# Two-layer decoder trunk: the norm's matrix of 1/1024 moved 64 bytes along its tile, and three 16-column products put ahead of query projections

## The chip, the cores and the metric

One core of a Trainium2 chip runs the whole program. The time is the device time of one execution in microseconds; for the kernel before, three executions gave 1483.13, 1483.56 and 1486.03 us, and the median is 1483.56 us. One more execution was profiled. In what follows PE is the matrix engine, DVE, ACT and POOL are the vector, scalar and GpSimd engines, and SP is the engine that issues most transfers.

## What is computed

A trunk of two layers over 512 tokens of width 1024, batch 1, all in float32. Each layer is a token mixer and a gated feed-forward network with a causal convolution; each of the two is led by an RMS norm that is shifted and scaled by a conditioning vector, and its output is gated and added to the residual stream. The first mixer is retention with four heads, the second an mLSTM with four heads; both have query and key width 256 and value width 512 per head.

```python
for i in range(DEPTH):
    h = rmsnorm(x, norm_tok_g[i]) * (1.0 + sc_t) + sh_t
    y = retention_mixer(h, ...) if i % 2 == 0 else mlstm_mixer(h, ...)
    x = x + gt_t * y
    h = rmsnorm(x, norm_ffn_g[i]) * (1.0 + sc_f) + sh_f
    x = x + gt_f * conv_ffn(h, ...)
return rmsnorm(x, final_g)
```

## The kernel before

**Products.** The residual stream lies in SBUF as eight tiles of 128 channels by 512 tokens. Every float32 operand of a large product is split into a rounded high part and a low part (names that end in h and l, or `whi` and `wlo`), and a product is three matmuls: high by high, high by low, low by high. Most large projections use a seven-product (Strassen-like) scheme: a matrix pair is cut in quarters and seven products of 128x256 columns in four steps take the place of eight (`ORDER`, `seven`, `fold_pairs`, `fold_values`). So the bulk of PE's work is matmuls of 256 moving columns; other stages (output projections, the first head's projections) use 512 columns, and the scores and their application mix 512, 384 and 256.

**Names on PE.** `p` is a folded projection, weights `whi` or `wlo` stationary and token tiles (`hh`, `hl`, `t24h`, `t3h`, ...) moving; `pv` is a folded value projection, token tiles stationary and weights moving; `po` is an output or down projection; `pf` are the first four products behind a norm; `psc` and `pav` are scores and their application; `pmu` and `pvar` are the two products of a head's group norm, with the matrix `ones_v`; `pms` are the two products of an RMS norm (or of its half), with the matrix `ones_d`, all entries 1/1024, stationary and the split sum of squares `ssh`, `ssl` moving.

**Where operands begin.** A token tile ("slot") is 512 words, 2048 bytes per partition, and is used from its first byte, or from its middle. A weight tile is 1024 + 64 words, 4352 bytes, and the folded weights, and those of the boundary at a norm, are used from word `OFF` = 16, 64 bytes in. `ones_d`, `ones_v` and `ones_1` are 128 words each and are used from their first byte; in the built program `ones_d` begins at byte 4352 of each partition, a multiple of 128.

**Boundaries.** At the end of a mixer or of a feed-forward network (`boundary`), the last output products run in two halves of 256 tokens, so that the first half's norm can start while the second half is multiplied. `Norm.root` issues the two `pms` products of a half. In three of the four boundaries the second half's `po` products are followed by `pf` (192 matmuls in four parts), and then by products of 512 columns; the fourth ends the program.

**A product nobody reads.** `short_product` multiplies the first weights of what follows with 16 columns into a place of PSUM that is written over later. It stands already ahead of the two mixers' last boundary (`contract_tiles` with `lead`) and ahead of the first folded unit of each feed-forward network (`folded`).

**Order.** The program is recorded as calls, and a planner (`Plan`) lists them engine by engine: PE's calls by their place in the code, the others by due times that it works out from PE's, with an estimate `occ` for each call. PE's order may still interleave the end of one seven-product group with the start of the next, where operands are late by the plan.

The lines that matter: `ones` at 431 to 436, `short_product` at 659, `seven` at 821, `fold_pairs` at 850, `ret_q` at 1714 and `ml_q` at 1856. All engine instructions are issued at line 383.

Of the kernel before, what the change touches and what calls it, by code (L numbers as in the profile page):

```python
# [11 lines left out]
F32R = mybir.dt.float32r  # L12
# [4 lines left out]
P = 128  # L17
# [18 lines left out]
WPAD = 64  # L36
OFF = 16
# [349 lines left out]
def trunk(ctx: ExitStack, tc: tile.TileContext, xT, cb, pos, vec, ident, decay, zmask, ada, w_s0, w_in0, w_v0,  # L387
          w_o0, w_in1, w_v1, w_f1, w_o1, w_up, w_dn, out):
    nc = tc.nc
    const = ctx.enter_context(tc.tile_pool(name="const", bufs=1))  # L390
# [10 lines left out]
    def uid(s):  # L401
        count[0] += 1
        return f"{s}_{count[0]}"

    def tile_of(pool, shape, dt, tag, name):
        return Buf(pool, shape, dt, tag, name, KINDS.get(tag, 0), tag == "ps")

    def slot(s, dt=F32, w=T):
        return tile_of(slots, [P, w], dt, "s", uid(s))
# [10 lines left out]
    def fixed(pool, shape, dt, name):  # L420
        b = tile_of(pool, shape, dt, name, name)
        b.get()
        return b

    plan = Plan()
    V, A, G, PE, S = (plan.engine(*p) for p in (("DVE", nc.vector), ("ACT", nc.scalar), ("POOL", nc.gpsimd),
                                                ("PE", nc.tensor), ("SP", nc.sync)))
# [3 lines left out]
    V.memset(fixed(const, [P, 32], F32, "pad")[:], 0.0)  # L431
    ones = {}
    for name, v in (("d", 1.0 / D), ("v", 1.0 / DV), ("1", 1.0)):
        o = fixed(const, [P, P], F32R, f"ones_{name}")
        V.memset(o[:].bitcast(F32), v)
        ones[name] = o

# [221 lines left out]
    def short_product(o, w, b):  # L659


        PE.matmul(o, w, b, start=True, stop=True, skip_group_check=True)

    def mm2(o, w, b, r=slice(None), start=True, stop=True):
        PE.matmul(o, w, b.hi[:, r], start=start, stop=False)
# [89 lines left out]
    def item(uses, fn, free=True):  # L755
        for u in uses:
            if u.first is None:
                u.first = len(items)
            u.last = len(items)
        items.append((uses, fn, free))  # L760
        steps_at.append(now[0])
# [3 lines left out]
    def proj_item(src, h, then, added=False):  # L765
        def fn(w):
            ps = bank("pp")
            for k in range(KT):
                cs = slice(k * P, k * P + P)
                mm3(ps[:], w[0].hi[:, cs], w[0].lo[:, cs], h[k].hi[:], h[k].lo[:], k == 0, k == KT - 1)  # L770
            then(ps)
        item([Use(src, KT * P, added=added)], fn)
# [45 lines left out]
                PE.matmul(o, b[0][:, ts], lo[:, cs], start=False, stop=False, skip_group_check=True)  # L818
                PE.matmul(o, b[1][:, ts], hi[:, cs], start=False, stop=sp, skip_group_check=True)

    def seven(use, streams, done, between=lambda j: None):


        fs = []

        def mk(n):
            def fn(w):
                if n == ORDER[0]:
                    for s in streams:
                        s.open(w[0])  # L830
                        fs.append(slot("fs"))
                for s, f in zip(streams, fs):
                    o = {1: s.c21, 2: s.c11, 5: s.c12, 3: s.c12}.get(n, s.c21)
                    s.product(n, o, n in s.starts)
                    if n in (1, 6, 7):
                        A.copy(f[:, HB if n == 6 else HA], s.c21)
                    if n == 7:
                        V.tensor_tensor(s.c22, s.c12, f[:, HA], op=ALU.add)
                    elif n == 2:
                        V.tensor_tensor(s.c11, s.c11, f[:, HA], op=ALU.add)  # L840
                    elif n == 3:
                        V.tensor_tensor(s.c12, s.c12, f[:, HB], op=ALU.add)
                if n == 3:
                    done(*[s.banks for s in streams])
            return fn
        for j, n in enumerate(ORDER):
            item([use], mk(n), j in FREE_STEPS)
            between(j)

    def fold_pairs(srcs, terms, thens, between=lambda j: None):  # L850

        def each(then):
            def done(bs):
                for b in bs:
                    then(b)
            return done
        for n, (src, then) in enumerate(zip(srcs, thens)):
            seven(FoldUse(src, n), [PairStream(terms, then)], each(then), lambda j: between(7 * n + j))

    def fold_values(src, terms, v, split, between=lambda j: None):  # L860

        def done(a, b):
            for ps in (a[0], b[0], a[1], b[1]):
                split(v, ps)
        seven(ValueFoldUse(src, 0), [ValueStream(terms, t) for t in range(2)], done, between)

    def folded(folds, h, terms, pairs, downs, quota):
# [30 lines left out]
        def unit(i):  # L898
# [10 lines left out]
            if i == 0:  # L909
                short_product(c2[:, HB][:, :16], folds[0].p[1][0][:, :P], terms(1, 0)[0][:, :16])  # L910
# [124 lines left out]
    def contract_tiles(w, n, gate, ys, i, t0, t1, after=lambda m: None, js=None, lead=False):  # L1035

        r = slice(t0, t1)
        per = WCOLS // (n * P)
        for j in js or range(per):
            m = i * per + j  # L1040
            ps = bank("po")
            if lead:
                short_product(ps[:, T - 16 :], w.hi[:, :P], ys(0).hi[:, :16])
                lead = False
            for k in range(n):
                cs = slice((j * n + k) * P, (j * n + k) * P + P)
                la = w.lo_at(j * n + k, k)
                mm3(ps[:, r], w.hi[:, cs], w.lo[:, la : la + P], ys(k).hi[:, r], ys(k).lo[:, r], k == 0, k == n - 1)
            add_residual(ps, m, gate(m), t0, t1)
            after(m)  # L1050
# [464 lines left out]
    def half_pair(st, name, finish):  # L1515

        got = []

        def then(ps):
            got.append(ps)  # L1520
            if len(got) == 2:
                st[name] = finish(*got)
        return then
# [181 lines left out]
    sums0 = Sums(h0, {}, 0, 0)  # L1705

    def sums_early():
        sums0.make()
        sums0.turn()

    def pair_srcs(w, at):
        return [(w[at], w[at + 1]), (w[at + 2], w[at + 3])]

    def ret_q(i, between=nothing):
        thens = [half_pair(R[i], name, rope) for name in ("q", "k")]
        if i:
            fold_pairs(pair_srcs(w_in0, i * 8), sums0.terms, thens, between)
            return
        for n, then in enumerate(thens):
            for j in range(2):  # L1720
                proj_item(w_in0[i * 8 + 2 * n + j], h0, then, 2 * n + j in QLOW)
        item([], lambda w: sums_early())

    def ret_g(i):
        fold_pairs(pair_srcs(w_in0, i * 8 + 4), sums0.terms, [ret_gate(i)] * 2)
# [9 lines left out]
    def ret_o(i):  # L1735
        if not i:
            item([], lambda w: load_x())
        return pieces(lambda j: w_o0[i, j], 4, gate_col(0, 0), lambda k: R[i]["y"][k], i in O_ADDED)

    ffn0 = Ffn(0)  # L1740
    heads(R, ret_q, ret_v, ret_scores, ret_g, ret_attend, lambda i: None, ret_end, ret_o,
          ffn0.start, RET_LAST, "ret")

# [41 lines left out]
    def conv_then(i, name, kt):  # L1785
        ch = (0 if name == "q" else 8) + i * 2 + kt

        def then(ps):
            acc = slot("mc")[:]
            c = lambda j: col("mcw", j * 16 + ch)  # L1790
            A.activation(acc, ps[:], AF.Identity, bias=col("mcb", ch), scale=c(3))
            for j, s in ((2, 1), (1, 2), (0, 3)):
                V.scalar_tensor_tensor(acc[:, s:], ps[:, : T - s], c(j), acc[:, s:], op0=ALU.mult, op1=ALU.add)
            A.activation(acc, acc, AF.Silu)
            M[i][name].append(pair_of("mqk", acc))
        return then
# [22 lines left out]
    def ml_gate(i):  # L1819
        def then(ps):  # L1820
            o = slot("o")
            A.activation(o[:], ps[:], AF.Sigmoid)
            M[i]["o"].append(o)
        return then
# [30 lines left out]

    def ml_q(i, between=nothing):
        thens = [lambda ps, name=name, n=iter((0, 1)): conv_then(i, name, next(n))(ps) for name in ("q", "k")]
        fold_pairs(pair_srcs(w_in1, 1 + i * 8), start1.sums.terms, thens, between)

    def ml_g(i):  # L1860
        fold_pairs(pair_srcs(w_in1, 5 + i * 8), start1.sums.terms, [ml_gate(i)] * 2)
# [4 lines left out]
    def ml_v(i, between=nothing):  # L1866
        fold_values(w_f1[i - 1], start1.sums.terms, M[i]["v"], plain_split, between)

    start1 = Start([w_in1[j] for j in (0, 5, 6, 7)], h1, 1, 0, [gates, ml_gate(0), ml_gate(0), ml_gate(0)], True)
# [3 lines left out]
    item([], lambda w: start1.sums.turn())  # L1873
    ffn1 = Ffn(1)
    heads(M, ml_q, ml_v, ml_scores, ml_g, ml_attend, lambda i: gn_center(M[i]), ml_end, ml_o,
          ffn1.start, ML_LAST, "ml")
    ffn1.items(End())
# [145 lines left out]
```

## Time and profile before

| what | value |
|---|---|
| median of three executions | 1483.56 us |
| profiled execution, its own time | 1483.41 us |
| its span, first to last instruction | 1481.6 us |
| granted PE clock, mean | 0.997 |
| busy: PE, DVE, ACT, POOL | 99%, 86%, 73%, 19% of the span |
| chain that ended last: PE, DMA, DVE | 86%, 7%, 3% |

The span is 1.8 us shorter than the execution's own time. Matmuls overlap in the profile: a matmul of 256 columns is shown as some 280 ns long, but the next one starts 113 to 118 ns after it. So in the timeline the difference between two start times, divided by the number of matmuls from the one to the other, tells what a matmul costs; the busy time does not. In the timeline a row is: start, length, engine, line, operation, output and inputs, stationary size, moving size and type, how many, and in brackets how long the engine was idle before it and who ended that.

### The profile page before, as it was taken

The numbers are of one execution on the slowest core, as the hardware profiler recorded it, in microseconds if no ns is written. First come the engines' busy times: TensorE is split into PE (matmuls) and PEld (weight loads), VectorE is DVE, ScalarE is ACT, GpSimd is POOL, SyncE is SP. The second block draws the span as 40 slices with busy tenths as digits, with TensorE's granted clock in tenths as the row PEclk, the third lists the DMA queues.
The fourth block names the chain that finished last, engine by engine and source line by source line (L and its number), as shares of the span: only waits on it lengthen the run. The fifth ranks groups of instructions, "written<-read, shape, count | busy, mean of one in ns | idle before, by whom it ended". The sixth has DMA issues, their size and how long they took to land.

```text
span 1481.6 us, 27248 instructions
## 1 busy us (share of the span) xinstructions
PE 1461.3 (99%) x10468; PEld 1368.8 (92%) x10468; DVE 1268.1 (86%) x2136; ACT 1075.9 (73%) x1606; POOL 279.0 (19%) x313
## 2 busy tenths in 40 slices
PE   9999999999999999999999999999999999999997
PEld 6799999998999999999999998999889899999997
DVE  7999979777989889898897999999889887777786
ACT  5678768777577676676668986989856876767662
POOL 0334132322111111111001222132211111111100
PEclk9999999999999999999999999999999999999998
DMA  9868989888798899999457895888687887888751
GB/s 363 252 175 207 282 209 230 224 250 212 206 215 215 241 261 258 265 261 266 118 180 171 207 246 144 208 221 199 205 239 201 213 219 194 194 208 191 190 125 58
DMA packets 93268, 315.65 MB, mean 213 GB/s; under 512 B 12225, under 2 KB 14657, under 8 KB 93138
## 3 DMA queue, kind: packets, MB, share of 16 engines
q0 software_dynamic: 32112, 116.54, 42.2%
q1 hardware_dynamic: 60738, 197.11, 38.3%
q8 instruction: 82, 1.34, 0.4%
q10 hardware_dynamic: 288, 0.27, 0.1%
q14 instruction: 48, 0.39, 0.1%
HBM read 195.23 MB, written 2.12 MB: 133 GB/s over the span
## 4 chain that ended last, share of the span: by engine, by line
PE 86%; DMA 7%; DVE 3%; ACT 2%; issue 2%; POOL 0%; DVEq 0%; ACTq 0%; SPq 0%; POOLq 0%
PE p L383 36%; PE po L383 27%; PE pv L383 9%; PE pav L383 4%; PE pp L383 3%; PE pf L383 3%; DMA wlo<-raw 2%; PE psc L383 2%; DMA raw<-w_in 1%; DMA wb<-w_up 1%; DMA raw<-w_dn 1%; PE pst L383 1%; DMA wlo<-wa 1%; DMA raw<-w_up 1%; PE pms L383 1%
## 5 line engine op out<-in xcount | busy, mean ns | idle before, releaser
L383 PE MATMUL p<-hh,whi 128*128 128x256 f32 (+1 forms) x994 | 275.6, 278 | 1.9 <-DVE p L383 1.9
L383 PE MATMUL p<-hl,whi 128*128 128x256 f32 x992 | 275.1, 277 | 0.0
L383 PE MATMUL p<-hh,wlo 128*128 128x256 f32 x992 | 273.4, 277 | 0.0
L383 ACT ACTIVATE wlo<-whi 128x1024 fp32r<-128x1024 f32 x223 | 235.0, 1057 | 39.8 <-PE po L383 15.1
L383 PEld LDWEIGHTS p<-hh,whi 128*128 128x128 f32 x994 | 187.1, 188 | 2.8 <-DVE p L383 2.3
L383 PEld LDWEIGHTS p<-hl,whi 128*128 128x128 f32 x992 | 186.7, 188 | 0.4
L383 PEld LDWEIGHTS p<-hh,wlo 128*128 128x128 f32 x992 | 185.6, 188 | 0.0
L383 PE MATMUL p<-t24h,whi 128*128 128x256 f32 x744 | 165.0, 279 | 4.1 <-ACT fs L383 3.1
L383 PE MATMUL po<-ggl,whi 128*128 128x512 f32 (+1 forms) x448 | 153.3, 343 | 0.0
L383 PE MATMUL po<-ggh,wlo 128*128 128x512 f32 (+1 forms) x448 | 153.1, 343 | 0.0
L383 PE MATMUL po<-ggh,whi 128*128 128x512 f32 (+1 forms) x448 | 152.4, 343 | 0.0
L383 ACT CAST whi<-raw 128x1024 fp32r<-128x1024 f32 (+1 forms) x117 | 118.0, 1019 | 44.8 <-DMA raw<-w_s 10.5
L383 PE MATMUL p<-t24l,whi 128*128 128x256 f32 x496 | 137.5, 277 | 0.0
L383 DVE SCALAR_TENSOR_TENSOR x<-po,mod,x 128x512 f32<-128x512 f32 (+1 forms) x184 | 113.0, 628 | 23.2 <-PE po L383 22.7
L383 PEld LDWEIGHTS p<-t24h,whi 128*128 128x128 f32 x744 | 126.3, 188 | 6.9 <-ACT fs L383 3.9
L383 DVE SCALAR_TENSOR_TENSOR ada<-ada,c_ext 128x1025 f32<-128x1025 f32 x96 | 119.5, 1246 | 6.5 <-DMA ada<-ada 6.4
L383 POOL DMA_DIRECT2D wlo<-wa x62 | 53.8, 867 | 355.4 <-ACT wlo L383 223.4
L383 PE MATMUL po<-yh,whi 128*128 128x256 f32 (+1 forms) x354 | 116.0, 329 | 0.3 <-ACT o L383 0.3
L383 PE MATMUL po<-yl,whi 128*128 128x256 f32 (+1 forms) x352 | 115.7, 329 | 0.0
L383 PE MATMUL po<-yh,wlo 128*128 128x256 f32 (+1 forms) x352 | 115.6, 329 | 0.0
L383 DVE SCALAR_TENSOR_TENSOR cv<-p,vecs,cv 128x511 f32<-128x511 f32 (+1 forms) x144 | 106.4, 744 | 9.9 <-ACT cv L383 9.2
L383 ACT CAST whi<-ws 128x1024 fp32r<-128x1024 f32 x86 | 90.0, 1050 | 28.5 <-DVE ws L383 23.5
(287 smaller groups left out, 4422.0 us busy)
## 6 DMA issues: line engine op xcount, KB each, us to landing
ada<-ada SPq DMA_DIRECT2D x96, 512.5 KB, 7.4
wlo<-ws POOLq DMA_DIRECT2D x68, 512.0 KB, 6.9
wlo<-wa POOLq DMA_DIRECT2D x62, 512.0 KB, 6.3
wlo<-wt POOLq DMA_DIRECT2D x44, 512.0 KB, 6.9
wlo<-raw POOLq DMA_DIRECT2D x41, 512.0 KB, 8.4
wa<-w_up SPq DMA_DIRECT2D x36, 512.0 KB, 6.9
wb<-w_up SPq DMA_DIRECT2D x36, 512.0 KB, 6.2
raw<-w_o SPq DMA_DIRECT2D x32, 512.0 KB, 6.6
```

The source lines that it names most:

```text
L383: getattr(c.obj, c.name)(*[real(v) for v in c.a], **{key: real(v) for key, v in c.k.items()})
```

## The change

`ones_d` becomes a tile of 128 + 64 words, of which words 16 to 143 are used: the matrix begins 64 bytes later. Every SBUF tile that is allocated behind it moves up by 256 bytes. `seven` takes a flag `lead`; where it is set, the first of the seven products is preceded by one 16-column product with its first high weights and its first moving tile, into the second bank's other half (`c22`), which is written by a vector instruction later on. The planner counts it with `occ = 0`. The flag is set for the first of the two groups in `ret_q(2)`, `ml_q(0)` and `ml_q(2)`: the third retention head's queries, and the first and third mLSTM heads' queries.

```diff
     for name, v in (("d", 1.0 / D), ("v", 1.0 / DV), ("1", 1.0)):
-        o = fixed(const, [P, P], F32R, f"ones_{name}")
+        off = OFF if name == "d" else 0
+        o = fixed(const, [P, P + WPAD * (off > 0)], F32R, f"ones_{name}")[:, off : off + P]
         V.memset(o[:].bitcast(F32), v)
...
-        PE.matmul(o, w, b, start=True, stop=True, skip_group_check=True)
+        return PE.matmul(o, w, b, start=True, stop=True, skip_group_check=True)
...
-    def seven(use, streams, done, between=lambda j: None):
+    def seven(use, streams, done, between=lambda j: None, lead=False):
...
                         s.open(w[0])
                         fs.append(slot("fs"))
+                    if lead:
+                        hi, hc, _, _ = w[0].p[n]
+                        short_product(streams[0].c22[:, :16], hi[:, hc : hc + P],
+                                      streams[0].terms(n, 0)[0][:, :16]).occ = 0.0
...
-            fold_pairs(pair_srcs(w_in0, i * 8), sums0.terms, thens, between)
+            fold_pairs(pair_srcs(w_in0, i * 8), sums0.terms, thens, between, i == 2)
...
-        fold_pairs(pair_srcs(w_in1, 1 + i * 8), start1.sums.terms, thens, between)
+        fold_pairs(pair_srcs(w_in1, 1 + i * 8), start1.sums.terms, thens, between, i in (0, 2))
```

On PE, at the start of `ret_q(2)`: the last two rows of the first head's output projection (`po`, 512 columns), and then the query products. This is a piece of the difference, with + for the row that is new.

```order
 L383 MATMUL po_2142<-yl_1916,whi_1880 128x512
 L383 MATMUL po_2142<-yh_1903,wlo_2021 128x512
+L383 MATMUL p_415_2161<-hh_239,whi_1842 128x16
 L383 MATMUL p_415_2161<-hh_239,whi_1842 128x256
 L383 MATMUL p_415_2161<-hl_267,whi_1842 128x256
```

One row is added, with the operands of the row behind it; nothing else moves there. On PE, at the start of `ml_q(2)`, behind the group norm's two products for the second mLSTM head (`pmu`), the kernel before has

```order
L383 MATMUL po_10997<-yh_10835,wlo_10896 128x512
L383 MATMUL pmu_11020<-zsh_10942,ones_v 128x512
L383 MATMUL pmu_11020<-zsl_10951,ones_v 128x512
L383 MATMUL p_1846_11028<-hh_8793,whi_10763 128x256
L383 MATMUL p_1846_11028<-hl_8805,whi_10763 128x256
```

and the changed kernel has (buffer numbers are higher by one for each product added ahead)

```order
L383 MATMUL po_10999<-yh_10837,wlo_10898 128x512
L383 MATMUL pmu_11022<-zsh_10944,ones_v 128x512
L383 MATMUL pmu_11022<-zsl_10953,ones_v 128x512
L383 MATMUL p_1846_11030<-hh_8794,whi_10765 128x16
L383 MATMUL p_1846_11030<-hh_8794,whi_10765 128x256
L383 MATMUL p_1846_11030<-hl_8806,whi_10765 128x256
```

Again one row is added. The third such row stands at the start of `ml_q(0)`, behind the first head's value products (`pv`, 512 columns). Apart from these three rows every engine has the same instructions in the same order as before, transfers included.

More of the change, by code (lines that the diff above doesn't have):

```diff
@@ L848, in seven, with fold_pairs @@
             between(j)
-    def fold_pairs(srcs, terms, thens, between=lambda j: None):
+    def fold_pairs(srcs, terms, thens, between=lambda j: None, lead=False):
         def each(then):
@@ L857, in fold_pairs @@
         for n, (src, then) in enumerate(zip(srcs, thens)):
-            seven(FoldUse(src, n), [PairStream(terms, then)], each(then), lambda j: between(7 * n + j))
+            seven(FoldUse(src, n), [PairStream(terms, then)], each(then), lambda j: between(7 * n + j),
+                  lead and not n)
     def fold_values(src, terms, v, split, between=lambda j: None):
```

## The prediction

> **What bounds the kernel now.** I read the page first: the span, and how much of it PE is busy.
>
> ```profile
> span 1481.6 us, 27248 instructions
> PE 1461.3 (99%) x10468; PEld 1368.8 (92%) x10468; DVE 1268.1 (86%) x2136; ACT 1075.9 (73%) x1606; POOL 279.0 (19%) x313
> L383 PE MATMUL p<-hh,whi 128*128 128x256 f32 (+1 forms) x994 | 275.6, 278 | 1.9 <-DVE p L383 1.9
> ```
>
> PE is the bound nearly everywhere, so what a matmul costs in time from start to start decides. That is read from PE's timeline, by the first and the last row of a stretch. The four rows below frame the 144 query products ahead of 159.42 (second retention head) and the 144 ahead of 208.62 (third head), the same kind of work.
>
> ```profile
> 143.10 0.28 PE L383 MATMUL p<-hh,whi 128*128 128x256 f32 x1
> ...
> 159.42 0.40 PE L383 MATMUL pav<-sh,vh 128*128 128x512 f32 x1
> ...
> 191.66 0.28 PE L383 MATMUL p<-hh,whi 128*128 128x256 f32 x1
> ...
> 208.62 0.28 PE L383 MATMUL pv<-whi,hh 128*128 128x256 f32 x1
> ```
>
> The first takes 16.32 us, **113.3 ns** a product, the second 16.96 us, **117.8 ns**, at the same clock and with no wait between. So a stream of 256-column products runs in one of two steps, 4.45 ns apart, and stays in it for long. What throws it from one into the other is what this change touches. First the norm's products:
>
> ```profile
> 387.45 0.28 PE L383 MATMUL po<-yh,whi 128*128 128x256 f32 x1
> ...
> 388.36 0.28 PE L383 MATMUL pms<-ssh,ones_d 128*128 128x256 f32 x1
> ...
> 389.07 0.28 PE L383 MATMUL po<-yh,whi 128*128 128x256 f32 x1
> ...
> 402.14 0.28 PE L383 MATMUL pf<-hh,whi 128*128 128x256 f32 x1
> 425.00 0.39 PE L383 MATMUL pp<-hh,whi 128*128 128x512 f32 x1
> ```
>
> The eight products before 388.36 take 0.91 us (114 ns each, as well as two decimals tell); the 111 from 389.07 to 402.14 take 13.07 us (117.7), and the 194 from there to 425.00 (192 `pf`, two `pms`) 22.86 us (117.8). The first `pms` turns fast into slow, and nothing turns it back before the 512-column products. Its neighbours have weights that begin 64 bytes into their tile and moving tiles that begin at byte 0; `ones_d` begins at byte 0 like its moving operand. The other boundaries have the same turn. Second, the unread product that the kernel has already:
>
> ```profile
> 368.40 0.39 PE L383 MATMUL po<-yh,wlo 128*128 128x512 f32 x1
> 368.63 0.40 PE L383 MATMUL po<-yh,whi 128*128 128x16 f32 x2
> ...
> 369.09 0.28 PE L383 MATMUL po<-yh,whi 128*128 128x256 f32 x1
> ```
>
> (The second row is two matmuls, 16 and 256 columns.) The stretch behind it is the fast one of the fence above. From 368.63 to 369.09, 0.46 us, stand the short product and three others, which would take 0.34 in fast steps: it **costs 0.12 us**, and is repaid after 27 products.
>
> **The norm's matrix (ones_d).** With the matrix 64 bytes in, `pms` has the byte offsets of its neighbours, and I take it that it passes like one of them. What then turns from slow to fast:
>
> ```profile
> 730.16 0.28 PE L383 MATMUL po<-ggh,whi 128*128 128x256 f32 x1
> ...
> 765.73 0.39 PE L383 MATMUL pp<-hh,whi 128*128 128x512 f32 x1
> ...
> 1117.27 0.28 PE L383 MATMUL po<-yh,wlo 128*128 128x256 f32 x1
> ...
> 1154.14 0.39 PE L383 MATMUL pp<-hh,whi 128*128 128x512 f32 x1
> ...
> 1457.86 0.28 PE L383 MATMUL po<-ggh,whi 128*128 128x256 f32 x1
> ...
> 1470.58 0.28 PE L383 MATMUL pms<-ssh,ones_d 128*128 128x256 f32 x1
> ```
>
> The program has 302, 313 and 108 products in these (35.57, 36.87 and 12.72 us, 117.8 each), and 310 from 388.48 to 425.00: 1033 x 4.45 ns = **4.60 us**. All lie on PE's path; the engine shows no wait in them. What may be late next are the weights of `pf`. Around 735 to 747 us, the view of the tile `wlo` has:
>
> ```profile
> L383 POOL DMA_DIRECT2D wlo<-raw x3: 862/1044/1102, 735.3 to 736.9; - x3
> DMA to landing us min/median/max: 5.5/9.6/12.4
> ```
>
> These low parts are made by adding transfers issued at 735.3 to 736.9; one of median length lands at 744.9 to 746.5, while `pf` starts at 742.88 and takes its third low part at 745.7. With PE 0.5 us earlier there and the transfer not, up to 0.5 us turns into a wait. I count it in full: 4.60 - 0.5 = **4.1 us**; without it 4.6.
>
> **The third retention head's queries.** The short product stands behind 512-column products in steady steps, as at 368.63, so I expect the same turn: 144 products at 113.3 in place of 117.8, 0.64 us less, plus 0.12, gives -0.52. What follows depends on the state that they leave. Rows of the stretches behind it, and of two others:
>
> ```profile
> 210.74 0.28 PE L383 MATMUL p<-t24h,whi 128*128 128x256 f32 x1
> 213.47 0.28 PE L383 MATMUL pv<-whi,hh 128*128 128x256 f32 x1
> 217.34 0.28 PE L383 MATMUL pv<-whi,t24h 128*128 128x256 f32 x1
> 231.47 0.39 PE L383 MATMUL psc<-qkh,qkh 128*128 128x512 f32 x1
> 281.19 0.28 PE L383 MATMUL p<-t24h,whi 128*128 128x256 f32 x1
> 284.02 0.28 PE L383 MATMUL pv<-whi,hl 128*128 128x256 f32 x1
> 294.49 0.28 PE L383 MATMUL pv<-whi,t3h 128*128 128x256 f32 x1
> 302.65 0.28 PE L383 MATMUL p<-hh,whi 128*128 128x256 f32 x1
> ```
>
> From `p` to `pv` the step stays (slow at 208.62, 18 products in 2.12 us). From `pv` to `p` it turns over: slow `pv` gives 24 fast `p` (210.74 to 213.47, 2.73 us), while at 281.19 the same 24 come behind fast `pv` and take 2.83. Two `pvar` between `pv` turn it too: fast before 217, slow after (120 in 14.13 us); the other way round at 294.49 (72 in 8.16 us, 113.3). So with a fast start: 18 `pv` -0.08, 24 `p` +0.10, 30 `pv` +0.13, `pvar` -0.01, 120 `pv` -0.53 us; the scores at 231.47 end it. Together **-0.91 us**. If only the 144 gained it would be -0.52, if everything to 231.47 were fast (282 products that are slow now) -1.13.
>
> **The first mLSTM head's queries.** Seventy products stand between the new row and a wait, shown in the timeline and in the chain of waits:
>
> ```profile
> 802.14 0.39 PE L383 MATMUL p<-t24h,whi 128*128 128x256 f32 x1 [0.66 <-DVE p L383]
> ```
>
> ```profile
> 793.15 5.98 DMA wb<-w_in
> ```
>
> The wait ends by a transfer and the DVE work behind it. The 70 x 4.45 ns - 0.12 us = 0.19 us that PE gains lengthens the wait: **0**, at best -0.19, and +0.12 if the turn fails and the wait didn't hide it.
>
> **The third mLSTM head's queries.**
>
> ```profile
> 919.23 0.28 PE L383 MATMUL p<-hh,whi 128*128 128x256 f32 x1
> 934.77 0.28 PE L383 MATMUL pv<-whi,hh 128*128 128x256 f32 x1
> 945.05 0.28 PE L383 MATMUL pv<-whi,t24h 128*128 128x256 f32 x1
> 958.65 0.39 PE L383 MATMUL psc<-mqkh,mqkh 128*128 128x512 f32 x1
> ```
>
> 132 products in 15.54 us, slow: -0.59 + 0.12 = -0.47. But here the turns work against it: one `pv` at 934.77, then 12 `p`, 13 `pv`, 24 `p`, 34 `pv`, two `pvar` and 120 `pv`, which run fast now (13.60 us). By the rules above they become slow: +0.53, and the short stretches between, each 4.45 ns a product, add +0.03, +0.06, -0.10, -0.15 and +0.01. Together **-0.1 us**. If the single `pv` doesn't turn the state, -0.47.
>
> **The sum.** -4.1 - 0.9 - 0 - 0.1 = -5.1 us against the profiled execution's own time of 1483.41 us, which is 0.15 below the median shown: **1478.3 us**.
>
> **Rivals.** *The matrix's place doesn't matter*: `pms` turns the stream for another reason, say its change of PSUM bank in mid-stream. For it speaks that `pms` differs from its neighbours in that too; against it, that `po` changes banks at every tile and stays fast up to 388. Then only -1.0 is left: 1482.4. The Trainium skill, "SBUF — State Buffer", section "Who interferes with whom", speaks for this rival: it gives PE two independent read ports, one for the moving operand and one for the weights, and by that where a matrix begins could not matter. The rows at 388.36 don't settle it, since they show the turn and not its cause.
>
> *Everything is kept*: no new wait at 745, the third mLSTM head keeps all, and the wait at 802 moves too: -4.6 - 0.9 - 0.2 - 0.5 = -6.2, 1477.2.
>
> *A new wait*: behind the norms, `pf` waits for the normed tiles and weights as long as it did, and only the `po` products between `pms` and `pf` gain: 115 + 108 + 118 + 108 = 449, 2.0 us, so -3.0, 1480.4.
>
> *The short products don't turn the stream*, so they only cost 2 x 0.12 (the one ahead of the wait is hidden): -4.1 + 0.24, 1479.6.
>
> *Slower*: all tiles behind `ones_d` move up by 256 bytes. If the fast step also hangs on a coarser address than 64 bytes, fast stretches turn slow. Price: a group of PE's in the first stretch of all above (143.3 to 159.3 us) and the same in the second (191.7 to 208.5) read
>
> ```profile
> L383 PE MATMUL p<-hh,whi 128*128 128x256 f32 x28 | 7.7, 276 | 0.0
> ```
>
> ```profile
> L383 PE MATMUL p<-hh,whi 128*128 128x256 f32 x28 | 7.9, 281 | 0.0
> ```
>
> so a `p` matmul is shown 276 ns long where fast and 281 where slow, and the page's mean of 278 makes some 60% of the program's 5208 fast; 3100 x 4.45 ns = 13.9 us, 1483.4 - 5.1 + 13.9 = 1492.2. It would be slower by 3 us from some 1800 such products. Against it: weight tiles are 4352 bytes apart, 256 off a multiple of 512, and fast stretches use one after the other.
>
> **How the numbers follow.** A measurement tells about 0.2% (3.0 us) from no change. Forecast 0.62, place doesn't matter 0.09, everything kept 0.12, a new wait 0.09, no turn by the short products 0.06, slower 0.02. Forecast, everything kept, a new wait and no turn make 0.89; with 0.3 us on either side for the spread of executions the range is 1476.9 to 1480.7, and I leave a tenth for what I haven't seen. Faster by over 0.2% is below 1480.6: 0.62 + 0.12 + 0.06 and some of the new wait, 0.83; within 0.2%: 0.15; slower 0.02.
>
> **What would show it.** In the changed profile: `po` behind the first `pms` of each boundary and `pf` at 113.3 ns from start to start; about 425 us into the span PE is 2.2 us earlier than now; a short wait or none at some 745; 144 query products near 190 at 113.3, then 24 at 117.8 behind the first `pv`, and 120 `pv` at 113.3; the wait at 802 longer by the gain ahead of it; 120 `pv` near 945 at 117.8. Wrong would be slow `po` behind `pms` (first rival), waits ahead of `pf` (third), slow query products behind the 16 columns (fourth), or 117.8 in places that have 113.3 now (last).

## The result and the profile after

The changed kernel takes **1480.83 us**, the median of 22 executions (1478.72 to 1483.72), against 1483.43 us for 22 of the kernel before (1478.49 to 1486.26): a ratio of 0.9985, 95% interval 0.9979 to 0.9992. That is 2.6 us less, where 5.1 us were forecast, and 0.13 us outside the range given. The profiled execution has 1479.65 us. Its page begins

```profile
span 1477.9 us, 27254 instructions
...
PE 1455.7 (98%) x10471; PEld 1364.2 (92%) x10471; DVE 1268.2 (86%) x2136; ACT 1075.0 (73%) x1606; POOL 278.7 (19%) x313
```

Three matmuls more, and 5.6 us less of busy PE. Below, rows are of the chain of waits where they have only an engine, a name and a count: start, length, the piece, and how many matmuls it holds. Length divided by count is the step. The first boundary, at 388 us:

```profile
388.64 0.11 PE pms L383
388.75 12.58 PE po L383 x111
401.33 3.40 PE pf L383 x30
...
405.30 0.22 PE pms L383
405.52 18.61 PE pf L383 x158
```

The 111 `po` behind `pms`, 13.07 us before, take 12.58: 113.3 ns each, as forecast. So do the 30 `pf` behind them. But the last 158 `pf` take 117.8, as before. Between them stands one `pms` that is 0.22 us long in place of 0.11. PE's timeline there, and below it DVE's:

```profile
405.03 0.28 PE L383 MATMUL pf<-hh,wlo 128*128 128x256 f32 x1
405.14 0.38 PE L383 MATMUL pms<-ssl,ones_d 128*128 128x256 f32 x1
405.36 0.28 PE L383 MATMUL pf<-hh,whi 128*128 128x256 f32 x1
```

```profile
404.67 0.41 DVE L383 TENSOR_TENSOR ssl<-ssq,ssh 128x256 fp32r<-128x256 f32 x1
```

DVE ends `ssl` at 405.08, some 0.06 us before the `pms` that reads it, which then lasts 0.38 us and not 0.28; the next step is 0.22 us. (Before the change the same two ended and began 0.36 us apart, shown further below.) The second boundary (timeline):

```profile
742.28 0.28 PE L383 MATMUL pf<-hl,whi 128*128 128x256 f32 x1
743.03 0.39 PE L383 MATMUL pf<-hh,wlo 128*128 128x256 f32 x1 [0.47 <-DMA wlo<-raw]
743.25 0.28 PE L383 MATMUL pf<-hh,whi 128*128 128x256 f32 x1
```

This is the wait for `wlo` that the prediction put at 745 by the old clock. From 742.28 to 743.25 are 0.97 us for two steps that take 0.23, so 0.74 us are lost. The third boundary, in the timeline and then in the chain:

```profile
1114.41 0.28 PE L383 MATMUL po<-yl,whi 128*128 128x256 f32 x1
1114.91 0.38 PE L383 MATMUL pms<-ssh,ones_d 128*128 128x256 f32 x1 [0.22 <-ACT ssh L383]
```

```profile
1115.86 12.92 PE po L383 x114
1128.78 3.51 PE pf L383 x30
...
1133.00 18.61 PE pf L383 x158
```

Here `pms` waits for `ssh`, made by ACT behind a row of DVE's additions. The 114 `po` behind it are still at 113.3, but `pf` falls to 117.8 after six products, at a matmul 0.12 us behind its neighbour (1129.30). The third retention head's queries (chain; the first piece holds the new product too):

```profile
192.33 16.45 PE p L383 x145
208.78 2.04 PE pv L383 x18
210.82 2.83 PE p L383 x24
213.65 3.54 PE pv L383 x30
217.18 0.47 PE pvar L383 x2
217.65 13.60 PE pv L383 x120
```

Steps of 113.3, 113.3, 117.9, 118 and 113.3 ns: the forecast sequence, piece by piece.

The table has, for each term, the time between the same two products in a profile of the changed kernel less that in the first profile of the kernel before. The changed kernel was profiled four times, first here and then as the runs "again", "again2" and "again3" below.

| term, us | forecast | first | again | again2 | again3 |
|---|---|---|---|---|---|
| `po` behind the first `pms`, four boundaries, with the wait at 1114 | -2.0 | -1.54 | -1.69 | -0.40 | -0.92 |
| `pf`, three boundaries, with the wait at 743 | -2.1 | -0.19 | -1.01 | -0.10 | -1.58 |
| `ret_q(2)` to the scores | -0.91 | -0.89 | -0.89 | -0.89 | -0.89 |
| `ml_q(0)` to the scores | 0 | +0.47 | +0.21 | +0.02 | +0.39 |
| `ml_q(2)` to the scores | -0.1 | -0.35 | -0.18 | -0.36 | -0.20 |
| sum | -5.1 | -2.50 | -3.56 | -1.73 | -3.20 |

The mean of the four sums is -2.75 us, close to what the medians say. The spans differ by more (-3.7 us for the first) through places that the change doesn't touch: two profiles of the kernel before ("before_again" below is the second) differ by 1.1 us. One wait near 450 us is 1.39 us shorter in the second. Against that, the products behind the wait at 802 us, the same 196 in both, take longer there (chain of the first, then of the second):

```profile
802.14 22.50 PE p L383 x196
```

```profile
801.23 23.35 PE p L383 x196
```

Behind a wait of 0.66 us the stream went on at 113.3 ns in the first, behind one of 0.63 us at 117.8 in the second, 0.85 us more for the same program.

### The profile page after: what moved, and what is told of

Read it like the earlier page. It is cut to its first block, busy times and chain, and to the rows that moved or that the text cites. A ratio compares the mean times of both kernels' runs of the same rounds, so it can differ in the third digit from the quotient of the medians.

```text
span 1477.9 us, 27254 instructions
## 1 busy us (share of the span) xinstructions
PE 1455.7 (98%) x10471; PEld 1364.2 (92%) x10471; DVE 1268.2 (86%) x2136; ACT 1075.0 (73%) x1606; POOL 278.7 (19%) x313
## 4 chain that ended last, share of the span: by engine, by line
PE 83%; DMA 7%; DVE 5%; ACT 3%; issue 2%; SPq 0%; POOL 0%; DVEq 0%; ACTq 0%; POOLq 0%
PE p L383 36%; PE po L383 23%; PE pv L383 8%; PE pp L383 4%; PE pav L383 4%; PE pf L383 4%; PE psc L383 2%; DMA ada<-ada 2%; DMA wlo<-raw 1%; DVE ada L383 1%; DMA raw<-w_dn 1%; DMA raw<-w_in 1%; DMA wb<-w_up 1%; ACT whi L383 1%; DVE x L383 1%
## 5 line engine op out<-in xcount | busy, mean ns | idle before, releaser
L383 ACT CAST whi<-raw 128x1024 fp32r<-128x1024 f32 (+1 forms) x117 | 117.9, 1019 | 51.4 <-DMA raw<-w_s 12.9
```

The costliest lines, as they stand in the source:

```text
L383: getattr(c.obj, c.name)(*[real(v) for v in c.a], **{key: real(v) for key, v in c.k.items()})
```

## The experiments

Times are medians, ratios are to the kernel before measured beside each group of runs (medians 1482.55, 1482.56, 1482.64 and 1482.24 us), with 95% intervals.

### The parts apart

"norm_only" has the matrix 64 bytes in and none of the three short products:

```diff
-            fold_pairs(pair_srcs(w_in0, i * 8), sums0.terms, thens, between, i == 2)
+            fold_pairs(pair_srcs(w_in0, i * 8), sums0.terms, thens, between)
-        fold_pairs(pair_srcs(w_in1, 1 + i * 8), start1.sums.terms, thens, between, i in (0, 2))
+        fold_pairs(pair_srcs(w_in1, 1 + i * 8), start1.sums.terms, thens, between)
```

> The matrix 64 bytes later, no new short products. Theory (the matrix's place turns the stream): the po products behind the first pms of all four boundaries run at 113.3 ns from start to start, 115, 108, 118 and 108 of them, 2.0 us less than before; pf runs at 113.3 only until a short wait of PE turns it, so between 0 and 2.6 us more; the query stretches at 191 and 919 us stay at 117.8. Time 2 to 3 us below the kernel before, ratio 0.998 to 0.9985. Rival (place doesn't matter, only the short products gained): po behind pms at 117.8, ratio 1.000.

Measured: 1479.52 us, 0.9985 (0.9976 to 0.9994).

"leads_pad" has the short products, and `ones_d` in a tile of the new width, from its first byte:

```diff
-        off = OFF if name == "d" else 0
-        o = fixed(const, [P, P + WPAD * (off > 0)], F32R, f"ones_{name}")[:, off : off + P]
+        wide_d = WPAD * (name == "d")
+        o = fixed(const, [P, P + wide_d], F32R, f"ones_{name}")[:, :P]
```

> The three short products, and the tile of the norm's matrix widened so that all tiles behind it move up by 256 bytes as in the change, but the matrix itself at byte 0. Theory: po behind pms at 117.8 ns in all four boundaries, as in the kernel before; 144 query products near 190 us at 113.3, with the turns behind them, -0.9 us; the first mLSTM head's 0 to +0.4 (its gain goes into the waits), the third's -0.35; ratio 0.9992 to 1.000. Rival (the shift by 256 bytes does it): po behind pms at 113.3 here too, ratio 0.998.

Measured: 1481.93 us, 0.9998 (0.9989 to 1.0007). In its chain the `po` behind the first `pms` read

```profile
388.25 13.07 PE po L383 x111
```

117.8 ns, as before the change; the other boundaries likewise. In "norm_only" they are at 113.3 in all four. The turn at `pms` is thus the place of the matrix and not the shift of the tiles behind it, nor `pms` itself. In "leads_pad" `ret_q(2)` gains its 0.89 us and in "norm_only" nothing, so the parts are separate. The time of "leads_pad" is no clean price of them, though: in its profile `pms` waits at 1114, and the stretch to `pf` there is 1.21 us longer than before.

"norm_only" also has no wait at 405 or 1114 ahead of a `pms`. There, by the chain,

```profile
406.78 17.91 PE pf L383 x158
...
1116.68 12.92 PE po L383 x114
...
1133.70 17.91 PE pf L383 x158
```

these stretches are at 113.3 to the end: -0.66 (`pf` at 402), -0.53 (`po` at 1117) and -0.86 us (`pf` at 1130). The last two are what the forecast had counted; the first is 0.2 us short by a wait at 402.9, which left 113.3. At 743 the wait for `wlo` left 117.8, and that `pf` is 0.65 us longer than before.

"again" is the changed kernel:

> The changed kernel once more, for a second profile. Theory (in pf a wait of some ten to hundred ns decides by chance of its length): po behind pms again at 113.3 in all four boundaries, while pf behind the mixers at 400 and 1129 us may come out otherwise than in the first profile, where both ran at 117.8 from their first small wait on; ratio 0.9975 to 0.9992. Rival (pf can't hold the step by its own pattern): pf goes to 117.8 in the same two places without a wait ahead of it.

Measured: 1479.58 us, 0.9983 (0.9974 to 0.9991).

### A short product inside pf

"pf_leads" adds an unread 16-column product in the first half of `pf`, ahead of its second part:

```diff
                 for k in range(k0, k1):
                     cs = slice(k * P, k * P + P)
+                if p == 0 and k0:
+                    PE.matmul(pss[0][:, 256:272], w[0].hi[:, k0 * P : k0 * P + P], h[k0].hi[:, :16], start=False, stop=False,
+                              skip_group_check=True).occ = 0.0
```

> The changed kernel with one more short product in each of the three pf stretches, ahead of the second quarter's first product (k = 4), into a part of the first bank that is written over later. Theory (a small wait leaves pf at 117.8, and a short product turns such a stream back): where pf is at 117.8 when the short product comes, the 144 products behind it run at 113.3, 0.64 - 0.12 = 0.52 us less at each of two places; where pf is at 113.3 already (near 745 us), it either stays (cost 0.12 us) or is turned to 117.8 (cost 0.6 us), which isn't known. Time 0.4 to 1.0 us below the changed kernel. Rival (pf can't hold the step by its own pattern): the 144 products stay at 117.8, time 0.4 us above the changed kernel.

Measured: 1479.95 us, 0.9982 (0.9974 to 0.9991): no gain over "again". Its timeline at 404 us:

```profile
404.10 0.28 PE L383 MATMUL pf<-hl,whi 128*128 128x256 f32 x1
404.21 0.28 PE L383 MATMUL pf<-hh,wlo 128*128 128x256 f32 x1
404.33 0.39 PE L383 MATMUL pf<-hh,whi 128*128 128x16 f32 x2
...
404.79 0.28 PE L383 MATMUL pf<-hh,wlo 128*128 128x256 f32 x1
404.91 0.28 PE L383 MATMUL pf<-hh,whi 128*128 128x256 f32 x1
```

The stream comes to it at 113.3 and leaves it at 117.8, to the end of `pf`. At 748 us the same happened, and at 1135 us, where it came at 117.8, it left at 113.3. So within 256-column products a short product **turned the step over** in all three places; it doesn't restore the lower one. (In this profile the `po` of the second boundary came to their `pms` at 117.8 already, from a step of 0.15 us at 708 on, and stayed there: the matrix's place keeps the step that the stream has.)

### A short product ahead of every query group

"lead_all" sets the flag in every `ret_q` and `ml_q`.

```diff
-            fold_pairs(pair_srcs(w_in0, i * 8), sums0.terms, thens, between, i == 2)
+            fold_pairs(pair_srcs(w_in0, i * 8), sums0.terms, thens, between, True)
-        fold_pairs(pair_srcs(w_in1, 1 + i * 8), start1.sums.terms, thens, between, i in (0, 2))
+        fold_pairs(pair_srcs(w_in1, 1 + i * 8), start1.sums.terms, thens, between, True)
```

> The changed kernel with the short product ahead of the query products of every head but the first retention head's, so of the second and fourth retention heads and of the second and fourth mLSTM heads too. Theory (the short product turns a stream over, whichever step it has): the 144 query products at 143 us, at 113.3 without it, run at 117.8, 0.64 + 0.12 = 0.76 us more; those at 869 us (113.3 without it) run at 117.8 up to the wait some 70 products on; the 108 at 1030 us, at 117.8 without it, run at 113.3, 0.48 - 0.12 = 0.36 us less. Rival (the gap that it makes restarts the stream at 113.3, whatever it had): the products at 143 and 869 us stay at 113.3, at a cost of 0.12 us each.

One execution: 1478.43 us. The expectation named some places wrongly: the added products stand at 88, 262, 806 and 986 us. The one at 806, behind fast queries of the first mLSTM head, turns them (timeline):

```profile
805.34 0.28 PE L383 MATMUL p<-t3h,whi 128*128 128x256 f32 x1
...
806.02 0.39 PE L383 MATMUL p<-hh,whi 128*128 128x16 f32 x2
...
806.37 0.28 PE L383 MATMUL p<-hh,wlo 128*128 128x256 f32 x1
...
807.43 0.28 PE L383 MATMUL p<-hh,wlo 128*128 128x256 f32 x1
```

Six products in 0.68 us ahead of it (113.3 ns), nine in 1.06 us behind (117.8). The one at 88, behind 512-column products, leaves 113.3; those at 262 and 986, behind score products of several widths, leave 117.8. In these profiles it left 113.3 every time only behind long 512-column stretches.

### Where in the tile the matrix must begin

"off128" and "off32" put the matrix 128 and 32 bytes into its tile:

```diff
-        off = OFF if name == "d" else 0
+        off = 2 * OFF if name == "d" else 0
```

(and `OFF // 2`).

> The changed kernel with the norm's matrix 128 bytes into its tile in place of 64. Theory (what counts is where in 128 bytes a matrix begins): po behind the first pms runs at 117.8 ns again at 388, 730 and 1457 us, in the changed kernel 113.3: 0.52, 0.49 and 0.49 us more. Rival (any other place than byte 0 will do, or an address coarser than 128 bytes counts): 113.3 as in the changed kernel.

> The changed kernel with the norm's matrix 32 bytes into its tile in place of 64. Theory (what counts is which 64-byte half of 128 bytes a matrix begins in): po behind the first pms runs at 117.8 as with byte 0. Rival (matrix and moving operand must only not begin at the same byte of 128): 113.3 as in the changed kernel, so 0.5 us less at each of 388, 730 and 1457 us than the kernel before.

One execution each: 1478.35 and 1479.02 us. The chain of "off32" reads

```profile
388.64 12.60 PE po L383 x111
...
1453.70 12.73 PE po L383 x108
```

At 388, where four `po` stand between the two `pms`, a few steps are longer and the stream comes back to 113.3 (0.02 us behind the 12.58 of 64 bytes). At 730 and 1457, where the two `pms` stand in a row, it stays at 117.8. "off128" does the same at all of these places (12.60, and 12.73 at 1453.03). So neither of the two expected patterns holds, that of a period of 128 bytes or that of any place but 0: of the four places tried, only 64 bytes, where the neighbours' weights begin too, passes without a trace. Whether it is the 64 or the likeness to the neighbours that counts was not tried.

### The waits ahead of pms

"pms_6" has the splits of the sum of squares planned to be ready 0.6 us earlier, so that `pms` comes a few products later on PE:

```diff
+                n = len(plan.calls)
                 self.parts.split(self.acc[:, r], r)
+                for c in plan.calls[n:]:
+                    c.lat += 0.6
```

> The changed kernel with the split sums of squares planned 0.6 us later, which moves the pms products some places back on PE (the low one of the second half at 405 us by one place, those of the first half by five to ten). Theory (PE's small wait for the low part at 405 us is what leaves pf at 117.8 there): without that wait pf holds 113.3 to its end, 0.6 us less at 402 to 425 us; at 1114 us no wait of PE for the high part, 0.3 to 0.5 us less. Time 0.5 to 1.5 us below the changed kernel, ratio to the kernel before 0.997 to 0.9985. Rival (pf loses the step by its own pattern): pf at 405 us at 117.8 without a wait, ratio as the changed kernel.

Measured: 1478.69 us, 0.9972 (0.9961 to 0.9983). But the waits were there still (steps of 0.18 us at `ssl` and 0.33 at `ssh`, in place of 0.11), so this kernel was measured again, with the changed kernel beside it:

> pms_6 once more, on the chip of again2. If putting pms some places later is worth something, its ratio is 0.0007 or more below that of again2; if its better ratio came from the chip and from how the waits fell, the two intervals overlap in most of their length.

> The changed kernel a third time, beside the next three on the same chip. Theory (the turns by the matrix and the short products are fixed; what a wait of PE leaves behind it differs from execution to execution): the same three gains as before, 0.92 us at 191 to 231 us and 0.5 each at 388, 730 and 1457; pf behind the mixers at 113.3 or 117.8 as it falls; ratio 0.998 to 0.9988.

Measured: 1479.74 us, 0.9980 (0.9971 to 0.9989), and for the changed kernel 1479.41, 0.9977 (0.9967 to 0.9986). No gain. The profile of "again2" shows how much chance there is. By its chain

```profile
405.54 0.22 PE pms L383
405.76 17.93 PE pf L383 x158
...
743.50 18.14 PE pf L383 x154
...
1115.19 13.43 PE po L383 x114
...
1132.86 18.61 PE pf L383 x158
```

and by its timeline

```profile
1114.21 0.39 PE L383 MATMUL pms<-ssh,ones_d 128*128 128x256 f32 x1 [0.83 <-ACT ssh L383]
```

The same wait at 405, 0.22 us, left 113.3 here and 117.8 in the first profile. The waits at 743 and 1114 left 117.8 here and 113.3 there.

"ret_lead" is the changed kernel without the two short products of the mLSTM heads (`False` in place of `i in (0, 2)`), and "before_again" is the kernel before:

> The changed kernel without the short products of the mLSTM's first and third head. Theory (the first one's gain of 0.19 us goes into the wait behind it, the third's is cut to about 0.2 by a turn some 68 products on): 0.2 us above again2, less than the interval. Rival (they gain what their 70 and 132 products have, 0.7 us): 0.5 to 0.7 us above again2.

> The kernel before, for a second profile of it, which shows how far two executions of one program differ place by place. Theory: the same steps (117.8 behind each pms, 117.8 at 191 us), but waits of PE at the start of the folded units (447 to 463 us, 1042 to 1062, 1176 to 1226) that differ from the first profile's by up to 1.4 us each.

Measured: 1478.08 us, 0.9973 (0.9961 to 0.9984), and 1482.27 us in one execution. The first ratio overlaps that of "again2" beside it, so what the mLSTM's products are worth can't be told from nothing by time. In the four boundaries, where no `po` and no `pf` waits in it, "before_again" has 117.8 wherever the first profile of before has it. Elsewhere the two differ, as behind the wait at 802.

The profile of "ret_lead" has no wait at 1114, and the profiles together say where that wait comes from. Some 26 us ahead of it DVE waits for a transfer, `ada<-ada`. DVE's timeline before, in "ret_lead" and in "again2":

```profile
1089.96 1.23 DVE L383 SCALAR_TENSOR_TENSOR ada<-ada,c_ext 128x1025 f32<-128x1025 f32 x1 [1.99 <-DMA ada<-ada]
```

```profile
1085.91 1.23 DVE L383 SCALAR_TENSOR_TENSOR ada<-ada,c_ext 128x1025 f32<-128x1025 f32 x1 [2.19 <-DMA ada<-ada]
```

```profile
1087.65 1.23 DVE L383 SCALAR_TENSOR_TENSOR ada<-ada,c_ext 128x1025 f32<-128x1025 f32 x1 [3.60 <-DMA ada<-ada]
```

In the five profiles in which this wait is 1.33 to 2.19 us (both of before, "norm_only", "ret_lead", "lead_all"), `pms` doesn't wait at 1114. In the eight that have 2.82 to 3.73 us and `pms` in its old place (the four of the changed kernel, "leads_pad", "off32", "off128", "pf_leads"), PE loses 0.31 to 1.21 us at 1114, each time DVE's wait less 2.50 us, to within 0.02. So `ssh` is late there because a transfer is, and not because the products at the boundary are faster: "leads_pad", whose matrix is at byte 0, loses most. The transfer is issued at the same point of the program and lands 9.4 to 10.3 us later in these eight, 7.9 to 8.8 us in the five. Every profile with the short products of just the first and third mLSTM heads has the longer time, and none without them; but "lead_all", which has them at all four heads, has 8.2 us. Why the transfer takes longer is open.

Last, the pair was put much further back, in the way of "pms_6" with 1.5 and 1.0 in place of 0.6:

> The changed kernel with the second half of the sum of squares planned 1.5 us later on PE: in the order the first pms of the two mixers' boundaries stands 13 and 11 po products further back than in the changed kernel, the second one 26 and 24, and the pair in pf stands at 31 and 50 (28 and 42) products in place of 30 and 35. Theory (short waits ahead of pms are what takes the missing part of the gain): the longest wait ahead of pms seen so far was 1.1 us, so 1.3 to 1.9 us leave none at 405 and 1114; po from 1117 and pf at 402 and 1131 run at 113.3 to their end. Against the profile of before those three stretches then give -0.65, -0.5 and -0.85 us, where the three profiles of the changed kernel gave -0.29, +0.28 and -0.30 on the mean: 1.7 us better than the changed kernel run beside it, a ratio of about 0.997 where that one has 0.998. The wait for wlo at 743 stays at 0.7 to 0.8 us. Rival (the waits only move): the later root makes the first half's normed tiles late, pf begins with a wait of 0.5 us or more, and the ratio is 0.998 or above. Second rival (the step turns without waits): no wait ahead of pms, and pf is still at 117.8 in one boundary or more.

> The same with 1.0 us in place of 1.5: the first pms stands 9 and 12 po products further back, the second 17 and 20, and the pair in pf at 28 and 46 products in all three boundaries that have one but the second. Theory: 1.0 to 1.4 us later is at the edge of the waits seen (up to 1.1 us at 1114, 0.22 us at 405), so none or a short one at 1114, none at 405; 1 to 1.7 us better than the changed kernel run beside it. Rival (the waits only move): no better than it.

> The changed kernel once more, for the two beside it: a ratio of 0.998 (0.9977 to 0.9985 so far); a wait at the second pms in pf at 405 (about 0.11 us lost), one at 743 (0.75 us) and one at 1114 (0.2 to 1.0 us), each with either step behind it.

Measured: 1486.24 us, 1.0014 (1.0004 to 1.0025); 1481.86 us, 0.9993 (0.9984 to 1.0003); and for the changed kernel 1478.01 us, 0.9967 (0.9954 to 0.9980). The expectation of a gain was wrong. In "pms_15" no `pms` waits, and where nothing else does, the streams hold 113.3; chain of the second boundary:

```profile
732.18 10.54 PE po L383 x93
...
749.13 15.91 PE pf L383 x140
```

But other waits come in their place (timeline of the third boundary):

```profile
1110.44 0.38 PE L383 MATMUL po<-yh,wlo 128*128 128x256 f32 x1 [1.47 <-DVE wlo L383]
...
1138.82 0.50 PE L383 MATMUL pf<-hh,whi 128*128 128x256 f32 x2 [0.80 <-ACT hh L383]
```

`pf` now waits for a normed tile, as the first rival to this expectation had it. (The profiled execution, 1487.87 us, is the longest of the twelve, which begin at 1480.96.) Behind the first of these waits, 106 `po` run at 117.8, and behind the second the last 151 `pf` at 113.3. The plan also put products of PE in another order: outside the first and third boundary, from 446 to 1100 us, it lost some 7 us against "again3". In "pms_10" a `pms` in `pf` still waits, with steps of 0.29 and 0.33 us at 405 and 1136. So the experiment says that the steps in these streams hold where nothing waits, and that taking these waits away through the plan's estimate only moves them. It doesn't say that every turn has a wait: at 1129.30 in the first profile a single step longer by 0.007 us is all that shows.

Counted over the profiles of all kernels with the matrix 64 bytes in but "pms_10" and "pms_15", at the three places where `po` or `pf` came at 113.3 to a wait (a step of 0.13 us or more that ends at a late operand):

| wait | how many | stream then at 113.3 | at 117.8 |
|---|---|---|---|
| at 405, `pms` for `ssl` | 5 | 3 | 2 |
| at 743, `pf` for `wlo` | 9 | 6 | 3 |
| at 1114, `pms` for `ssh` | 7 | 4 | 3 |

21 waits, 8 of which left the higher step. The lengths don't tell them apart: at 743 they are steps of 0.73 to 0.78 us ahead of 113.3 and of 0.76 to 0.78 ahead of 117.8, at 1114 of 0.31 to 1.10 and of 0.33 to 1.10. Not in the table are four waits at 402 us, at the seventh `pf` (steps of 0.21 to 0.24 us, in "again3", "lead_all", "norm_only" and "ret_lead"); all four left 113.3.

## Why the prediction was right and wrong

**The matrix's place: right.** At 64 bytes `pms` passes like a neighbour (12.58 us for 111 `po`), at byte 0 of the same wide tile it doesn't (13.07), and the kernel with that is no faster than before (0.9998). The rival by which the place doesn't matter falls. The rule that stood behind it, that of the Trainium skill's "SBUF — State Buffer", section "Who interferes with whom", by which PE reads weights and moving operand through independent ports, would give both runs the same step if read as the prediction reads it; the 111 `po` differ by 0.49 us. The rival of the 256-byte shift falls by the same run, which has the shift: apart from the turn forecast at 211 us, the one longer stretch that went from 113.3 to 117.8 against the first profile of before is 72 `pv` at 294 us, and these are at 117.8 in "before_again" too, without the shift.

**`ret_q(2)`: right to 0.02 us**, forecast -0.91, measured -0.89, with every turn as worked out.

**`ml_q(0)`: right in that no gain reaches the scores** (+0.02 to +0.47). In the first profile the 70 products run at 113.3, with one step of 0.4 us among them at 792.38, and the wait behind them is longer:

```profile
799.31 0.39 PE L383 MATMUL p<-t24h,whi 128*128 128x256 f32 x1 [0.92 <-DVE p L383]
```

0.92 us where it was 0.66. In the other three it is 0.67, 0.88 and 0.64, and two of them have the long step at 792 too. "ret_lead", without the product, has that step as well (0.43) and comes to the scores 0.65 us later than before, so the plus can't be put down to the product.

**`ml_q(2)`: right in sum, wrong in its course.** Forecast -0.1, measured -0.18 to -0.36. The 132 queries turned as expected, but after some 70 came one to four steps near 0.12 us, behind which "again" and "again3" went on at 117.8 and the other two fell back to 113.3. And the 120 `pv` near 945 stayed at 113.3 in every profile (13.60 us in "again2"), where the rules of turning said 117.8. The rule that failed is that `pv` to `p` turns the step over: the 24 `p` behind the 13 `pv` took 2.83 us behind slow `pv` (1.53 us, first profile) as behind fast ones (1.47, before), and from there all ran as before the change.

**What failed is the term 1033 x 4.45 ns, and of it the step "All lie on PE's path; the engine shows no wait in them. What may be late next are the weights of `pf`."** The term had two parts. The 449 `po` were to bring 2.0 us; they are at 113.3 in the four boundaries unless a wait comes first, but at 1114 PE waits for `ssh`, which costs 0.3 to 1.1 us in all four profiles of the table, and in "again2" the step behind it too. The other 584, `pf` and its `pms`, were to bring 2.1 net of the wait for `wlo`; they brought 0.1 to 1.6. Two things were left out.

First, what is late next is not only `wlo` but also `ssl` and `ssh`, the operands of the very products that were mended. The profile of before had it to be read. Its timeline of DVE, and that of PE, at the first boundary:

```profile
405.50 0.41 DVE L383 TENSOR_TENSOR ssl<-ssq,ssh 128x256 fp32r<-128x256 f32 x1
```

```profile
406.27 0.28 PE L383 MATMUL pms<-ssl,ones_d 128*128 128x256 f32 x1
```

`ssl` was early by 0.36 us (405.91 to 406.27). In the changed kernel's profile the `pms` comes 1.13 us sooner (405.14), 145 products x 4.45 ns = 0.65 of it by the step from 388 on, while `ssl` ends only 0.83 us sooner (405.08). At 1114 the operand is `ssh`, made by 1116.81 and read at 1117.15 before the change. The cause of that wait is another: the transfer `ada<-ada` that DVE waits for some 26 us earlier (2.82 to 3.60 us in the four profiles, 1.99 before), and not the step.

Second, a wait can cost more than its length. 0.11 us lost at 405 were followed by 158 products at 117.8, another 0.70 us. The prediction took the step as a property that a stretch keeps, and said so of 512-column products, `pms`, `pv` and 16 columns; that a short wait is one more thing that can turn it wasn't among them, though the unread products had shown that a break in the rhythm of some 0.1 us is enough.

**The wait for `wlo`** came where it was put (743, by the old clock 745.7) and cost 0.74 us instead of up to 0.5.

The rival "a new wait" came out nearest by number (1480.4 against 1480.83). Its mechanism was that `pf` waits as long as it gains; what was seen is half of that: some waiting, and more loss by the step behind it. The four measurements of the changed kernel (0.9985, 0.9983, 0.9977, 0.9967) fit a gain of 2.2 to 4.9 us, of which each wait decides some 0.7 us (158 products at 405) to 1.4 us (311 at 1114 in "again2") anew in every profile; the kernel before has such a wait too, at 802.

What stays open: what decides the step behind a wait, which its length alone doesn't, and why the transfer `ada<-ada` takes longer. And no kernel here was shown to beat the changed one: "pms_6", second time round, and "ret_lead" overlap with it where all three were measured side by side.

## What to carry to other kernels

Read the step from start to start over a whole stretch; where two steps appear at one clock, find the product at which they turn, and compare its operands' places with its neighbours'. Before counting a gain over everything behind that product, list what each operand of the stretch was early by: an engine that comes 0.5 us sooner meets them all, and an operand's maker may itself wait for a transfer. And where a step can be lost at a wait, weigh a wait by what follows it (158 x 4.45 ns) and not by its length alone.

## What the runs showed of the hardware

- The step of a 256-column stream depends on where a single product's weights begin: with byte 0 among neighbours at 64 the stream goes on at 117.8 in place of 113.3 ns; at 32 and 128 bytes (one profile each) a lone one disturbs a few steps and two in a row turn it.
- The step outlives its cause: 158 products took 18.61 us (405 us, first profile) or 17.93 ("again2"), at a granted clock of 1.00 in both.
- A 16-column product among 256-column ones turns 113.3 to 117.8 (404, 748 and 806 us) as readily as 117.8 to 113.3 (1135 us), and only behind long stretches of 512 columns did it always leave 113.3.
- Of 21 waits in streams at 113.3, 13 left 113.3 and 8 left 117.8, at the same three places. The kernel before shows it too: behind the wait at 802 the same 196 products took 22.50 us in one execution and 23.35 in another.
